# The last expert's rows joined to the final norm in PSUM, and the slots of extra rows made one step earlier

## The chip, the cores and the metric

One core of a Trainium2 chip runs one program. The metric is the device time of an execution in microseconds (us), shown as the median of three runs. All times below are of the kernel before, unless the text says otherwise.

## The reference

An encoder block on 1024 tokens of width 1024: time mixing and attention, then a top-4-of-32 expert layer, and a layer norm after each. Only its last part matters here:

```python
ffn = _moe(h, router_w, router_b, exp_w1, exp_b1, exp_w2, exp_b2)
h = _layer_norm(DEEPNORM_ALPHA * h + ffn, ln2_w, ln2_b)
# for each expert e and the rows xb that chose it:
hid = xb @ w1[e] + b1[e]                       # 1024 -> 2048
act = x_glu * sigmoid(1.702 * x_glu) * (x_lin + 1)   # both halves clamped
out = (act @ w2[e] + b2[e]) * gate             # 1024 -> 1024, summed over the experts of a token
```

## The kernel before, in words

**The expert stage** (`experts`) takes some 1,520 us of the program. The 32 experts are ranked by how many rows they got, and stand in a fixed order of places, `SEQ` (L42). The 18 fullest (ranks below `NH`) have room for 160 rows, 128 and 32 extra ones; the other 14 have room for 128. A place with room for extra rows is called an x place here, and the others plain. `SEQ` mixes both; with x for an x place and a dot for a plain one it reads `x.x.x.xx.x.x.x.xx.x.x.xx.x.x.xx.`. Rows beyond an expert's room go to a loop at the end (`For_i`, L1383) over blocks of left-over rows; its count comes from a register.

The stage runs in 32 windows. **Window r** is `up` of place r (8 blocks of weights, each with 12 products of 128x512 into the PSUM tile `h`) and then `down` of place r-1 (4 blocks, each with 12 products into `o`). Weights arrive as fp32 in a ring of six 1 MB buffers `raw`, and ACT and DVE split each block into a high part `wh` (a cast, L1177) and a low part `wl` (a subtraction, L1180). Extra rows have fp32 products of their own into `ex`: after every second block, eight of them at a time (L1198, L1253).

The small work is hung on 12 steps of a window, in a table `jobs` that is written by hand: step s comes after up block s (0 to 7) or after down block s-8 (8 to 11). An engine does its part in the order in which the steps are called. What matters here:

- Steps 8 and 9: the two halves of the activation of place r (`gm`, `lm` on DVE, `sm` on ACT), L1215 to L1219.
- Step 8 (`SLP` = -4), after the first half: `slots` for place r+2. PE makes the table of row numbers with one-hot products into a PSUM tile of tag `tr`; DVE copies it out as `sv` (and `st`, the extra rows' part) and works out the indices of the gather that POOL issues.
- Step 10 (`SLP + SLE` with `SLE` = 2), if place r+2 is an x place: `extra` (L1023). PE turns `st` with one product, `slots<-ident,st` (L1026), again into a `tr` tile, and DVE copies it out as a second `sv` (L1004).
- Step 11 and steps 1 and 2 of the next window (`TP`): the activation is transposed by PE into `tr` tiles (L1145, L1240), which ACT casts (`ah`) and DVE subtracts from (`al`, L1148).

There is one buffer of tag `tr`, so each of its users on PE waits until the one before has been copied out.

**The end of the stage.** `down` scales the rows by their gate (ACT, L1271) and POOL adds them to `ya_d` in DRAM with an indirect DMA (L1272; the extra rows L1281). These additions wait for one another. After window 31 comes `down` of the last place, alone, and then the loop over left-over blocks, at whose head all engines meet after every DMA has landed.

**The final norm** (`final_norm`) reads `ya_d` in eight tiles `fy` of 128x1024 and `ln2`'s weight and bias. DVE takes the statistics (L1444, L1446), subtracts the mean and multiplies by the weight (L1448), and works out the reciprocal root with a chain of small operations for two tiles at a time (L288 to L302). For five tiles ACT multiplies by the root (L1434) and POOL adds the bias (L1435); for the tiles in `FV` DVE does both (L1432).

Of the kernel before, what the change touches and what calls it, by code (L numbers as in the profile page):

```python
# [18 lines left out]
P = 128  # L19
# [19 lines left out]
CAP = P + CX  # L39
NH = 18  # L40

SEQ = (0, *sorted(range(1, NE - 1), key=lambda r: (r + 0.5) / NH if r < NH else (r - NH + 0.5) / (NE - NH)), NE - 1)  # L42

FIRST = 10
XP = (4, 5, 7)
TP = (11, 13, 14)
SLP = -4
SLE = 2
S1 = 1
MP = 6  # L50
DP = 8
# [1 line left out]
EH = 3  # L53

XB = 2
FG = (0, 2, 4, 6, 8)
FV = (4, 6, 7)
HB = 2
SB = 3
PB = 2  # L60
# [11 lines left out]
def hybrid_kernel(ctx: ExitStack, tc: tile.TileContext, A, out):  # L72
# [204 lines left out]
    ps3_.__exit__(None, None, None)  # L277
    p3_.__exit__(None, None, None)
    experts(tc, A, dict(locals()))
    final_norm(tc, A, dict(locals()))  # L280


def rsqrt_steps(nc, pool, v, n, scale, eps, name="rq", out=None):
# [830 lines left out]
def experts(tc, A, L):  # L1114
# [3 lines left out]
    with ExitStack() as cx:  # L1118
        wr = L["wr"]
        ep = cx.enter_context(tc.tile_pool(name="ep", bufs=1, reuse_waits="tile"))  # L1120
        wp = cx.enter_context(tc.tile_pool(name="wp", bufs=1, side="right", reuse_waits="tile"))
        pq = cx.enter_context(tc.tile_pool(name="pq", bufs=1, space=PS, reuse_waits="tile"))
        bh, ioc, select, pr = (L[k] for k in ("bh", "ioc", "select", "pr"))
        o = ep.tile([P, D], FT, name="o")
        ox = ep.tile([CX, 2, 512], FT, name="ox")
        def record(e, xtra):
            n = CAP if xtra else P
            pv = ep.tile([P, NT, 8], BF, name="pv", bufs=2)
            sp.dma_start(pv, L["val_d"][bass.ds(e, 1)].rearrange("e p t c -> p (e t) c"))
            return pv, n  # L1130

        def mark(pv, n, pos):
            oh = ep.tile([P, NT, CAP], BF, name="oh")[:, :, :n]
# [29 lines left out]

        stream, raws, highs, ready = [], L["raws"], L["highs"], []

        def weights(j, ahead):

            while len(raws) < min(j + RB, len(stream)):
                raw = wr.tile([P, 2 * FF], FT, name="raw", bufs=RB)
# [12 lines left out]
            return ready[j]  # L1182

        def up(j0, sel, xh, xl, xt, step=lambda s: None):
            ps = pq.tile([P, 4, 512], FT, name="h")
            px = pq.tile([P, 512], FT, name="ex") if xt is not None else None
            cols = [slice(512 * c, 512 * c + 512) for c in range(4)]
            for c, m in enumerate(cols):
                pe.matmul(ps[:, c], sel, bh[:, m], start=True, stop=False)

            def extra(k, raw):
                if px is None:
                    return
                if k == 0:
                    for c, m in enumerate(cols):
                        pe.matmul(px[32 * c:32 * c + 32], sel[:, 0:CX], bh[:, m], start=True, stop=False)
                for c, m in enumerate(cols):
                    pe.matmul(px[32 * c:32 * c + 32], xt[:, k], raw[:, m], start=False, stop=(k == KD - 1))  # L1198

            late = []  # L1200
            for k in range(KD):
                raw, h, l = weights(j0 + k, AH[xt is not None])
# [41 lines left out]
        def down(j0, ah, al, ax, gate, idx, step=lambda s: None):  # L1244
# [9 lines left out]

            late = []
            for b in range(4):
                raw, h, l = weights(j0 + b, AH[ax is not None])
                for kk in range(2):
                    k = 2 * b + kk
                    for x, w, z in ((ah, h, False), (ah, l, False), (al, h, k == KD - 1)):  # L1260
# [6 lines left out]
                        extra(*x)  # L1267
                    late.clear()
                step(KD + b)
            o = ep.tile([P, D], FT, name="o")  # L1270
            ac.activation(o, po.rearrange("p c n -> p (c n)"), AF.Copy, scale=gate[:, 0:1])  # L1271
            gp.indirect_dma_start(out=ya_d, out_offset=bass.IndirectOffsetOnAxis(ap=idx[:, 0:1], axis=0), in_=o, in_offset=None, compute_op=OP.add)  # L1272
            if px is None:
                return
# [31 lines left out]
        def begin2(r):  # L1306
            pv, n = info[r]
            info[r] = (pv, mark(pv, n, pv[:, :, 6:7]), n, select(L["pick"][:, SEQ[r]:SEQ[r] + 1]))

        def begin3(r, xs=None):  # L1310
            pv, oh, n, sel = info[r]
# [7 lines left out]
        def plan(r, where, f):  # L1319
            jobs.setdefault(12 * r + where, []).append(f)  # L1320
# [13 lines left out]
        with tc.manual_schedule():  # L1334
# [48 lines left out]
        with tc.For_i(0, n, 1) as i:  # L1383
            ei = ep.tile([1, 1], I32, name="ei")
            sp.dma_start(ei, L["tabi_d"][bass.ds(i, 1), :])
            row = L["tab_d"][bass.ds(i, 1), :]
# [14 lines left out]
            raws.clear()  # L1401
            highs.clear()
            ready.clear()
            parts, turns, a = act(*up(0, select(pick), *x))
            run_all(parts + turns)
            down(KD, *a, gate, idx)


def final_norm(tc, A, L):
    nc = tc.nc  # L1410
    ve, ac, gp, sp = nc.vector, nc.scalar, nc.gpsimd, nc.sync
    ya_d, bcast, out = L["ya_d"], L["bcast"], L["out"]
    with tc.tile_pool(name="fn", bufs=1, reuse_waits="tile") as fp:
        ys = [fp.tile([P, D], FT, name=f"fy{t}") for t in range(NT)]
        w = fp.tile([P, D], FT, name="l2w")
        b = fp.tile([P, D], FT, name="l2b")
        for t in range(NT):
            sp.dma_start(ys[t], ya_d[t * P:(t + 1) * P, :])  # L1418
            if t == 0:
                sp.dma_start(w, bcast(A["ln2_w"], D))  # L1420
            elif t == 4:
                sp.dma_start(b, bcast(A["ln2_b"], D))
        mv = fp.tile([P, NT, 2], FT, name="fmv")
        st = fp.tile([P, NT, 2, 6], FT, name="fst")
        def chain(g0, g1):
            return rsqrt_steps(nc, fp, mv[:, g0:g1, 1], g1 - g0, 1.0, LN_EPS, name=f"f{g0}")

        def last(g0, g1, r):
            for t in range(g0, g1):
                rt = r[:, t - g0:t - g0 + 1]  # L1430
                if t in FV:
                    ve.scalar_tensor_tensor(ys[t], ys[t], rt, b, op0=OP.mult, op1=OP.add)  # L1432
                else:
                    ac.activation(ys[t], ys[t], AF.Copy, scale=rt)  # L1434
                    gp.tensor_tensor(ys[t], ys[t], b, op=OP.add)  # L1435
                sp.dma_start(out[t * P:(t + 1) * P, :], ys[t])

        with tc.manual_schedule():
            run = None
            for g0, g1 in zip(FG, FG[1:]):  # L1440
                for t in range(g0, g1):
                    for i in range(4):
                        if i < 2:
                            ve.bn_stats(st[:, t, i], ys[t][:, 512 * i:512 * i + 512])  # L1444
                        elif i == 2:
                            ve.bn_aggr(mv[:, t], st[:, t])  # L1446
                        else:
                            ve.scalar_tensor_tensor(ys[t], ys[t], mv[:, t, 0:1], w, op0=OP.subtract, op1=OP.mult)  # L1448
                        if run is not None and next(run[0], run) is run:
                            last(*run[1:])  # L1450
                            run = None
                if run is not None:
                    for _ in run[0]:
                        pass
                    last(*run[1:])
                c = chain(g0, g1)
                run = (c, g0, g1, next(c))
            for _ in run[0]:
                pass
            last(*run[1:])  # L1460


def L_lor(lor, which):
# [55 lines left out]
```

## Time and profile before

| | us |
|---|---|
| median of 3 runs (2611.49 to 2621.80) | 2618.14 |
| the profiled execution | 2618.31 |
| its span | 2616.6 |
| PE busy | 2376.1 (91%) |
| DVE busy | 1940.6 (74%) |
| ACT busy | 1319.8 (50%) |
| POOL busy | 415.6 (16%) |
| mean granted TensorE clock | 0.961 of full speed |

The rows further down are of that profiled execution. In a view of time a row is: start, duration, engine, line of the kernel, operation, out<-in, sizes, count; a bracket at its end tells how long the engine had been idle and which instruction ended that. PE is the matmul engine and PEld its weight load; SPq is a DMA that SyncE's queue issues. In a view by stretches PEclk is the granted clock: 1.00 is 2.4 GHz and 0.50 is 1.2 GHz.

### The profile page before, as it was taken

The numbers are of one execution on the slowest core, as the hardware profiler recorded it, in microseconds if no ns is written. First come the engines' busy times: TensorE is split into PE (matmuls) and PEld (weight loads), VectorE is DVE, ScalarE is ACT, GpSimd is POOL, SyncE is SP. The second block draws the span as 40 slices with busy tenths as digits, with TensorE's granted clock in tenths as the row PEclk, the third lists the DMA queues.
The fourth block names the chain that finished last, engine by engine and source line by source line (L and its number), as shares of the span: only waits on it lengthen the run. The fifth ranks groups of instructions, "written<-read, shape, count | busy, mean of one in ns | idle before, by whom it ended". The sixth has DMA issues, their size and how long they took to land. (4 is left out here: it accounts for less than half of the span.)

```text
span 2616.6 us, 37332 instructions
## 1 busy us (share of the span) xinstructions
PE 2376.1 (91%) x14029; PEld 1793.9 (69%) x14029; DVE 1940.6 (74%) x2901; ACT 1319.8 (50%) x1606; POOL 415.6 (16%) x370
## 2 busy tenths in 40 slices
PE   5999998998989996899999999999999999999991
PEld 5778998977766664656666666666666666666660
DVE  8367344377886687778788887887878888788786
ACT  3354332354344333546556566565655656556561
POOL 4300211122131011011111011110211102102002
PEclk9999999999999996999999999999999999999995
DMA  6323864217537325677877779777897778977774
GB/s 225 130 81 143 278 204 71 93 51 255 172 125 268 111 86 180 259 261 277 323 286 286 298 272 339 283 258 294 305 337 273 272 284 310 330 277 266 287 276 155
DMA packets 184649, 607.14 MB, mean 232 GB/s; under 512 B 69961, under 2 KB 95689, under 8 KB 130834
## 3 DMA queue, kind: packets, MB, share of 16 engines
q1 hardware_dynamic: 155874, 525.24, 54.3%
q0 software_dynamic: 17600, 65.55, 9.0%
q10 hardware_dynamic: 10992, 13.93, 1.7%
q8 instruction: 112, 1.84, 0.3%
q14 instruction: 71, 0.58, 0.1%
HBM read 518.64 MB, written 86.02 MB: 231 GB/s over the span
## 5 line engine op out<-in xcount | busy, mean ns | idle before, releaser
L1180 DVE TENSOR_TENSOR wl<-raw,wh 128x2048 fp32r<-128x2048 f32 x384 | 876.1, 2289 | 223.3 <-ACT wh L1177 222.7
L1177 ACT CAST wh<-raw 128x2048 fp32r<-128x2048 f32 x381 | 720.9, 1905 | 127.5 <-DMA raw<-w 78.6
L1205 PE MATMUL h<-wh,xh 128*128 128x512 f32 x1024 | 307.5, 423 | 1.0 <-ACT wh L1177 1.0
L1205 PE MATMUL h<-wl,xh 128*128 128x512 f32 x1024 | 285.5, 401 | 1.1 <-DVE wl L1180 1.1
L1205 PE MATMUL h<-wh,xl 128*128 128x512 f32 x1024 | 281.1, 396 | 0.0
L1205 PEld LDWEIGHTS h<-wl,xh 128*128 128x128 f32 x1024 | 196.5, 192 | 49.3 <-DVE wl L1180 1.6
L1205 PEld LDWEIGHTS h<-wh,xh 128*128 128x128 f32 x1024 | 189.2, 195 | 56.0 <-issue 12.3
L1205 PEld LDWEIGHTS h<-wh,xl 128*128 128x128 f32 x1024 | 193.6, 189 | 47.1
L1009 POOL DMA_INDIRECT xg<-h_d,idx x32 | 70.4, 2202 | 955.9 <-PE ex L1253 307.6
L153 PE MATMUL mm<-whi,hT_lo 128*128 128x256 f32 x640 | 186.6, 293 | 10.4 <-DVE hT_lo L182 5.4
L151 PE MATMUL mm<-whi,hT_hi 128*128 128x256 f32 x640 | 186.9, 293 | 5.3 <-ACT sq L487 3.6
L152 PE MATMUL mm<-wlo,hT_hi 128*128 128x256 f32 x640 | 185.6, 291 | 0.0
L1263 PE MATMUL o<-wh,ah 128*128 128x512 f32 x512 | 170.9, 415 | 0.0
L1263 PE MATMUL o<-wl,ah 128*128 128x512 f32 x512 | 161.4, 396 | 0.0
L1263 PE MATMUL o<-wh,al 128*128 128x512 f32 x512 | 161.3, 396 | 0.0
L1216 ACT ACTIVATE sm<-gm 128x512 f32<-128x512 f32 x64 | 40.4, 632 | 199.8 <-DVE gm L1215 199.8
L1198 PE MATMUL ex<-raw,xt 128*32 128x512 f32 x1152 | 139.7, 603 | 0.0
L153 PEld LDWEIGHTS mm<-whi,hT_lo 128*128 128x128 f32 x640 | 126.2, 197 | 12.3 <-DVE hT_lo L182 6.6
L151 PEld LDWEIGHTS mm<-whi,hT_hi 128*128 128x128 f32 x640 | 126.5, 198 | 8.6 <-ACT sq L487 4.0
L152 PEld LDWEIGHTS mm<-wlo,hT_hi 128*128 128x128 f32 x640 | 126.3, 197 | 0.0
L1263 PEld LDWEIGHTS o<-wh,ah 128*128 128x128 f32 x512 | 89.1, 188 | 42.4 <-issue 25.1
L1263 PEld LDWEIGHTS o<-wh,al 128*128 128x128 f32 x512 | 96.4, 188 | 23.3
(421 smaller groups left out, 4154.3 us busy)
## 6 DMA issues: line engine op xcount, KB each, us to landing
raw<-w SPq DMA_DIRECT2D x384, 1024.0 KB, 7.0
pks<-pk_d SPq DMA_DIRECT2D x16, 1152.0 KB, 6.0
pk_d<-pk POOLq DMA_DIRECT2D x16, 896.0 KB, 5.4
h_d<-h SPq DMA_DIRECT2D x17, 512.0 KB, 2.6
raw<-w_fx ACTq DMA_DIRECT2D x8, 1024.0 KB, 5.4
fx_d<-fraw POOLq DMA_DIRECT2D x64, 128.0 KB, 2.8
qkvo<-fx_d SPq DMA_DIRECT2D x32, 256.0 KB, 6.1
x<-x SPq DMA_DIRECT2D x8, 512.0 KB, 3.8
```

The source lines that it names most:

```text
L151: pe.matmul(ps, hi[:, k, n], whi[:, k], start=(k == 0), stop=False)
L152: pe.matmul(ps, hi[:, k, n], wlo[:, k], start=False, stop=False)
L153: pe.matmul(ps, lo[:, k, n], whi[:, k], start=False, stop=(k == KD - 1))
L1009: gp.indirect_dma_start(out=x, out_offset=None, in_=h1_d, in_offset=bass.IndirectOffsetOnAxis(ap=idx[0:m, i:i + 1], axis=0))
L1177: ac.copy(highs[i], raw)
L1180: ve.tensor_tensor(l, raw, f32(h), op=OP.subtract)
L1198: pe.matmul(px[32 * c:32 * c + 32], xt[:, k], raw[:, m], start=False, stop=(k == KD - 1))
L1205: pe.matmul(ps[:, c], x[:, k], w[:, m], start=False, stop=z)
L1216: ac.activation(sg, g, AF.Sigmoid, scale=SWI)
L1263: pe.matmul(po[:, c], x[:, k], w[:, m], start=(k == 0 and x is ah and w is h), stop=z)
```

## The change

1. **`extra` moves from step 10 to step 9** (`SLE` = 1), and stands in front of what step 9 already held, the second half of the activation.
2. **The order of places**: the plain place of rank 30 moves to place 30, right before the last, which is plain too, and the others are mixed again. In the same signs the order is now `x.x.xx.x.xx.x.xx.x.xx.x.xx.x.x..`.
3. **The last place's rows are not added to `ya_d`.** They stay in SBUF (`kept[:, S:]`). PE turns the place's one-hot table `oh` (8 products with a bf16 unit matrix `idb`, copied out by ACT into `oht`), in front of the last `down`. The final norm then makes each tile in PSUM: two fp32 products of `ident` with the tile of `ya_d`, and two of `oht` with the kept rows, 128x512 each.
4. **The reads of `ya_d` move** in front of the last `down`, into four of the six `raw` buffers (`sums`, four DMAs of 1 MB), with the weight and the bias of the norm before them. They must follow the additions of place 30. The loop over left-over blocks is then in front of the norm; inside it, each turn reads the sums again.
5. **The norm itself**: DVE reads the tile from PSUM in three places (statistics twice, subtraction); the chain works in a PSUM tile `ch`, takes three, three and two tiles (`FG`), and has the factor -1/8192 moved into the weight (ACT, once). DVE finishes tiles 6 and 7 (`FV`) with the bias from PSUM, and ACT and POOL the other six.

```diff
-SEQ = (0, *sorted(range(1, NE - 1), key=lambda r: (r + 0.5) / NH if r < NH else (r - NH + 0.5) / (NE - NH)), NE - 1)
+SEQ = (0, *sorted(range(1, NE - 2), key=lambda r: (r + 0.5) / NH if r < NH else (r - NH + 0.5) / (NE - 2 - NH)), NE - 2, NE - 1)
-SLE = 2
+SLE = 1
-FG = (0, 2, 4, 6, 8)
-FV = (4, 6, 7)
+FG = (0, 3, 6, 8)
+FV = (6, 7)
...
                     if SEQ[r] < NH:
-                        plan(r - 1, (S1 if r == 1 else SLP) + SLE, extra)
+                        jobs.setdefault(12 * (r - 1) + (S1 if r == 1 else SLP) + SLE, []).insert(0, extra)
...
-            down(at["d", NE - 1], *prev)
+            ring = lambda: wr.tile([P, 2 * FF], FT, name="raw", bufs=RB)
+            kept = ring()
+            oht = kept[:, :S].rearrange("p (t q) -> p t q", t=NT)
+            for g in range(2):
+                ps = pq.tile([P, 4, P], FT, name="tr")
+                for j in range(4):
+                    pe.matmul(ps[:, j], last_oh[0][:, 4 * g + j], idb, start=True, stop=True)
+                ac.copy(oht[:, 4 * g:4 * g + 4], ps)
+            wb = ring().rearrange("p (i d) -> p i d", i=2)
+            for i, nm in enumerate(("ln2_w", "ln2_b")):
+                sp.dma_start(wb[:, i], L["bcast"](A[nm], D))
+            ys = [ring().rearrange("p (t d) -> p t d", t=2) for _ in range(NT // 2)]
...
+            sums()
+            down(at["d", NE - 1], *prev, o=kept[:, S:])
...
+    ac.activation(w, w, AF.Copy, scale=-1.0 / 8192.0)
+    def bring(t):
+        y = pt.tile([P, 2, 512], FT, name="y", bufs=3)
+        for c in range(2):
+            q = slice(512 * c, 512 * c + 512)
+            pe.matmul(y[:, c], ident, ys[t][:, q], start=True, stop=False)
+        for c in range(2):
+            q = slice(512 * c, 512 * c + 512)
+            pe.matmul(y[:, c], oht[:, t], o[:, q], start=False, stop=True)
+        return y
...
+    for g0, g1 in zip(FG, FG[1:]):
+        for t in range(g0, g1):
+            y = bring(t)
+            for c in range(2):
+                ve.bn_stats(st[:, t, c], y[:, c])
+                advance()
+            ve.bn_aggr(mv[:, t], st[:, t])
+            advance()
+            ve.scalar_tensor_tensor(ys[t], y.rearrange("p c n -> p (c n)"), mv[:, t, 0:1], w, op0=OP.subtract, op1=OP.mult)
+            advance()
+        advance(True)
+        run = (chain(g0, g1), g0, g1)
+        next(run[0])
```

`advance` does one small operation of the earlier group's chain, and calls `finish` (scale, bias, DMA out) when the chain has ended.

What the table does to the order is seen best on DVE, in `down` of a window whose place r+2 is an x place (L1215 to L1219 are one half of the activation, `wl` the low part of the next weights). Before:

```order
L1219 TENSOR_TENSOR lm<-lm,sm 128x512 [waits DVE_49,Activation_49]
L1029 COPY st<-slots 6x128 [waits PE_49]
L1004 COPY sv<-slots 128x6
...
L1180 TENSOR_TENSOR wl<-raw,wh 128x2048 [waits DMAHW7_49,Activation_49]
L1215 TENSOR_SCALAR gm<-h 128x512
L1217 TENSOR_SCALAR lm<-h 128x512
L1218 SCALAR_TENSOR_TENSOR lm<-lm,gm 128x512 [waits DVE_49]
L1219 TENSOR_TENSOR lm<-lm,sm 128x512 [waits DVE_49,Activation_49]
L1180 TENSOR_TENSOR wl<-raw,wh 128x2048 [waits DMAHW0_49,Activation_49]
L1004 COPY sv<-slots 128x6 [waits PE_49]
```

Now (L1028 is `st`, L1003 `sv`, L1187 `wl`, L1222 to L1226 the activation):

```order
L1226 TENSOR_TENSOR lm<-lm,sm 128x512 [waits DVE_49,Activation_49]
L1028 COPY st<-slots 6x128 [waits PE_49]
L1003 COPY sv<-slots 128x6
...
L1187 TENSOR_TENSOR wl<-raw,wh 128x2048 [waits DMAHW4_49,Activation_49]
L1003 COPY sv<-slots 128x6 [waits DVE_49,PE_49]
...
L1222 TENSOR_SCALAR gm<-h 128x512
L1224 TENSOR_SCALAR lm<-h 128x512
L1225 SCALAR_TENSOR_TENSOR lm<-lm,gm 128x512 [waits DVE_49]
L1226 TENSOR_TENSOR lm<-lm,sm 128x512 [waits DVE_49,Activation_49]
L1187 TENSOR_TENSOR wl<-raw,wh 128x2048 [waits DMAHW5_49,Activation_49]
```

The second `sv` has moved in front of the second half of the activation and of one `wl`.

On PE the product that waits for `st` and the transposes that need its `tr` tile stand in the same `down`; each block of weights is six pairs of products. Before, the three blocks ahead of it:

```order
L1263 MATMUL o<-wh,al 128x512 x2
L1263 MATMUL o<-wh,ah 128x512 x2
L1263 MATMUL o<-wl,ah 128x512 x2
L1263 MATMUL o<-wh,al 128x512 x2
L1026 MATMUL slots<-ident,st 128x6 [waits DVE_49,PE_49]
L1263 MATMUL o<-wh,ah 128x512 [waits Activation_49]
...
L1263 MATMUL o<-wh,al 128x512 x2
L1145 MATMUL tr<-ident,lm 128x128 [waits DVE_49]
```

Now, two blocks ahead of it and two behind:

```order
L1270 MATMUL o<-wh,al 128x512 x2
L1025 MATMUL slots<-ident,st 128x6 [waits DVE_49,PE_49]
L1270 MATMUL o<-wh,ah 128x512 [waits Activation_49]
...
L1270 MATMUL o<-wh,ah 128x512 [waits Activation_49]
...
L1270 MATMUL o<-wh,al 128x512 x2
L1149 MATMUL tr<-ident,lm 128x128 [waits DVE_49]
```

The product stands one block earlier on PE, and the transposes have one block more between it and them.

At the end of the stage, PE's rows between the last transposes of the activation and the last `down` are new:

```order
L1149 MATMUL tr<-ident,lm 128x128 [waits DVE_49]
L1149 MATMUL tr<-ident,lm 128x128 x3
L1399 LDWEIGHTS oh
L1399 MATMUL tr<-idb,oh 128x128 [waits DVE_49]
...
L1399 MATMUL tr<-idb,oh 128x128 [waits Activation_49]
...
L1270 MATMUL o<-wh,ah 128x512 x2
```

Each group of four waits until the `tr` tile before it has been copied out, by DVE and then by ACT.

## Rows read from the trace of the kernel before

**Rows 1.** The waits of PE: engine, line <- releaser: total us, times, longest.

```profile
PE tr L1145 <- DVE sv L1004: 45.5, 13, 4.8
...
PE tr L1240 <- DVE al L1148: 6.4, 4, 1.7
```

**Rows 2.** PE in time, the `down` of window 13 and the next `up`.

```profile
1504.27 0.63 PE L1263 MATMUL o<-wh,ah 128*128 128x512 f32 x2
...
1515.04 1.11 PE L1145 MATMUL tr<-ident,lm 128*128 128x128 f32 x4 [4.50 <-DVE sv L1004]
...
1524.93 0.60 PE L1145 MATMUL tr<-ident,lm 128*128 128x128 f32 x4
```

**Rows 3.** DVE in time, the same stretch.

```profile
1506.61 0.14 DVE L1004 COPY sv<-slots 128x6 f32<-128x6 f32 x1
...
1514.83 0.15 DVE L1004 COPY sv<-slots 128x6 f32<-128x6 f32 x1
```

**Rows 4.** All engines in time, window 5 (place 5 plain, 4 x).

```profile
1315.21 1.92 PE L1253 MATMUL ex<-raw,ax 128*32 128x512 f32 x16
...
1316.18 0.14 DVE L1004 COPY sv<-slots 128x6 f32<-128x6 f32 x1
```

**Rows 5.** PE in time, windows 7 (places 7 and 6 both x) and 8.

```profile
1421.29 0.66 PE L1145 MATMUL tr<-ident,lm 128*128 128x128 f32 x4 [0.61 <-DVE sv L1004]
...
1428.26 0.60 PE L1145 MATMUL tr<-ident,lm 128*128 128x128 f32 x4
...
1433.23 0.44 PE L1240 MATMUL tr<-ident,lx 128*128 128x128 f32 x2 [1.57 <-DVE al L1148]
```

**Rows 6.** Stretches from a wait's end on: us, PE busy, PEclk, DMA share, GB/s.

```profile
1186.50:1193.50 7.00, 7.00 (x26) 0.76 0.88 305
1515.00:1522.00 7.00, 6.96 (x20) 0.55 0.91 312
...
1433.20:1440.20 7.00, 6.97 (x33) 1.00 1.03 399
...
2545.60:2552.60 7.00, 6.95 (x26) 0.77 0.50 77
```

**Rows 7.** All engines in time, from window 31's end to the end.

```profile
2545.65 1.11 PE L1145 MATMUL tr<-ident,lm 128*128 128x128 f32 x4 [2.22 <-DVE al L1148]
...
2548.08 0.69 DVE L1148 TENSOR_TENSOR al<-tr,ah 128x512 fp32r<-128x512 f32 x1
...
2558.29 0.63 PE L1263 MATMUL o<-wh,al 128*128 128x512 f32 x2
2558.96 1.11 ACT L1271 ACTIVATE o<-o,gate 128x1024 f32<-128x1024 f32 x1 [9.16 <-PE o L1263]
...
2567.36 0.35 SPq L1418 DMA_DIRECT2D fy<-ya_d  x1
...
2570.99 1.29 DVE L1444 BATCH_NORM_STATS2 fst<-fy 128x6 f32<-128x512 f32 x2 [18.86 <-DMA fy<-ya_d]
...
2610.40 2.48 DVE L1432 SCALAR_TENSOR_TENSOR fy<-fy,f_r,l2b 128x1024 f32<-128x1024 f32 x2
```

**Rows 8.** POOL and DVE in time, the norm.

```profile
2595.50 4.63 POOL L1435 TENSOR_TENSOR fy<-fy,l2b 128x1024 f32<-128x1024 f32 x2 [5.92 <-ACT fy L1434]
...
...
2597.78 3.44 DVE L1448 SCALAR_TENSOR_TENSOR fy<-fy,fmv,l2w 128x1024 f32<-128x1024 f32 x1
...
2602.84 1.28 DVE L1448 SCALAR_TENSOR_TENSOR fy<-fy,fmv,l2w 128x1024 f32<-128x1024 f32 x1
```

**Rows 9.** PE in time, two fp32 products of 128x512 (L444, four records) behind another.

```profile
157.49 0.39 PE L146 MATMUL mm<-hT_hi,wlo 128*128 128x512 f32 x1
157.72 1.88 PE L444 MATMUL qk<-kn,bdones 128*128 128x512 f32 x4
```

**Rows 10.** POOL and DVE in time, an earlier stage: an addition beside one with a PSUM input.

```profile
929.96 2.36 POOL L328 TENSOR_TENSOR h<-h,p3lb 128x1024 f32<-128x1024 f32 x1 [21.12 <-DVE h L327]
...
930.25 0.67 DVE L908 TENSOR_TENSOR u<-u,mm 128x512 f32<-128x512 f32 x1
```

More of the change, by code (lines that the diff above doesn't have):

```diff
@@ L279, in hybrid_kernel @@
     experts(tc, A, dict(locals()))
-    final_norm(tc, A, dict(locals()))
 def rsqrt_steps(nc, pool, v, n, scale, eps, name="rq", out=None):
@@ L1121, in experts @@
         wp = cx.enter_context(tc.tile_pool(name="wp", bufs=1, side="right", reuse_waits="tile"))
-        pq = cx.enter_context(tc.tile_pool(name="pq", bufs=1, space=PS, reuse_waits="tile"))
+        pq_ = tc.tile_pool(name="pq", bufs=1, space=PS, reuse_waits="tile")
+        pq = pq_.__enter__()
+        idb = ep.tile([P, P], BF, name="idb")
+        ve.tensor_copy(idb, ident)
         bh, ioc, select, pr = (L[k] for k in ("bh", "ioc", "select", "pr"))
@@ L1130, in record @@
             return pv, n
+        last_oh = []
         def mark(pv, n, pos):
@@ L1164, in experts @@
         stream, raws, highs, ready = [], L["raws"], L["highs"], []
+        src = ["raw", RB, RB]
         def weights(j, ahead):
-            while len(raws) < min(j + RB, len(stream)):
-                raw = wr.tile([P, 2 * FF], FT, name="raw", bufs=RB)
+            while len(raws) < min(j + src[1], len(stream)):
+                raw = wr.tile([P, 2 * FF], FT, name="raw", tag=src[0], bufs=src[2])
                 sp.dma_start(raw, stream[len(raws)]())
@@ L1201, in up @@
             for k in range(KD):
-                raw, h, l = weights(j0 + k, AH[xt is not None])
+                raw, h, l = weights(j0 + k, AH[xt is not None] if src[0] == "raw" else 0)
                 for x, w, z in ((xh, h, False), (xh, l, False), (xl, h, k == KD - 1)):
@@ L1242, in act, with down @@
             return [extra, lambda: half(0), lambda: half(1)], turns + [piece], (ah, al, ax)
-        def down(j0, ah, al, ax, gate, idx, step=lambda s: None):
+        def down(j0, ah, al, ax, gate, idx, step=lambda s: None, o=None):
             po = pq.tile([P, 2, 512], FT, name="o")
@@ L1256, in down @@
             for b in range(4):
-                raw, h, l = weights(j0 + b, AH[ax is not None])
+                raw, h, l = weights(j0 + b, AH[ax is not None] if src[0] == "raw" else 0)
                 for kk in range(2):
@@ L1269, in down @@
                 step(KD + b)
-            o = ep.tile([P, D], FT, name="o")
+            keep = o is not None
+            if not keep:
+                o = ep.tile([P, D], FT, name="o")
             ac.activation(o, po.rearrange("p c n -> p (c n)"), AF.Copy, scale=gate[:, 0:1])
+            if keep:
+                return
             gp.indirect_dma_start(out=ya_d, out_offset=bass.IndirectOffsetOnAxis(ap=idx[:, 0:1], axis=0), in_=o, in_offset=None, compute_op=OP.add)
@@ L1308, in begin2 @@
             info[r] = (pv, mark(pv, n, pv[:, :, 6:7]), n, select(L["pick"][:, SEQ[r]:SEQ[r] + 1]))
+            if r == NE - 1:
+                last_oh.append(info[r][1])
         def begin3(r, xs=None):
@@ L1378, in experts, with sums @@
                 step(NE, s)
-            down(at["d", NE - 1], *prev)
+            ring = lambda: wr.tile([P, 2 * FF], FT, name="raw", bufs=RB)
[10 more added lines that the diff above has]
+            ys = [ring().rearrange("p (t d) -> p t d", t=2) for _ in range(NT // 2)]
+            def sums():
+                for g, y in enumerate(ys):
+                    sp.dma_start(y, ya_d[2 * g * P:2 * (g + 1) * P, :].rearrange("(t p) d -> p t d", p=P))
+            sums()
+            down(at["d", NE - 1], *prev, o=kept[:, S:])
+            pq_.__exit__(None, None, None)
         n = nc.values_load(L["tot"][0:1, 0:1], min_val=0, max_val=NE)
         with tc.For_i(0, n, 1) as i:
+            pq_ = tc.tile_pool(name="pq2", bufs=1, space=PS, reuse_waits="tile")
+            pq = pq_.__enter__()
             ei = ep.tile([1, 1], I32, name="ei")
@@ L1403, in experts @@
             ready.clear()
+            src[:] = "wh", 2, WB
             parts, turns, a = act(*up(0, select(pick), *x))
@@ L1406, in experts @@
             down(KD, *a, gate, idx)
-def final_norm(tc, A, L):
-    nc = tc.nc
[L1411 to L1460, printed above, removed]
@@ new lines, in experts, with final_norm, chain, finish @@
+            sums()
+            pq_.__exit__(None, None, None)
+        with tc.manual_schedule(), tc.tile_pool(name="pt", bufs=1, space=PS, reuse_waits="tile") as pt:
+            final_norm(tc, A, L, ep, pt, wb, [y[:, t] for y in ys for t in range(2)], oht, kept[:, S:])
+def final_norm(tc, A, L, ep, pt, wb, ys, oht, o):
+    nc = tc.nc
+    ve, ac, pe, gp, sp = nc.vector, nc.scalar, nc.tensor, nc.gpsimd, nc.sync
+    out, ident = L["out"], L["ident"]
+    w, b = wb[:, 0], wb[:, 1]
+    ac.activation(w, w, AF.Copy, scale=-1.0 / 8192.0)
+    mv = ep.tile([P, NT, 2], FT, name="fmv")
+    st = ep.tile([P, NT, 2, 6], FT, name="fst")
+    rr = ep.tile([P, NT], FT, name="frr")
+    def bring(t):
[7 more added lines that the diff above has]
+        return y
+    def chain(g0, g1):
+        n = g1 - g0
+        tl = pt.tile([P, 2, 8], FT, name="ch")
+        a, t = (tl[:, i, 0:n] for i in range(2))
+        r = rr[:, g0:g1]
+        ve.tensor_scalar(a, mv[:, g0:g1, 1], LN_EPS, None, op0=OP.add)
+        yield
+        ve.tensor_scalar(r.bitcast(I32), a.bitcast(I32), -0.5, 1597463007.0, op0=OP.mult, op1=OP.add)
+        yield
+        for c in (3.0, 12.0, 768.0):
+            ve.tensor_tensor(t, a, r, op=OP.mult)
+            yield
+            ve.tensor_tensor(t, t, r, op=OP.mult)
+            yield
+            ve.scalar_tensor_tensor(r, t, c, r, op0=OP.subtract, op1=OP.mult)
+            yield
+    def finish(g0, g1):
+        for t in range(g0, g1):
+            rt = rr[:, t:t + 1]
+            if t in FV:
+                ve.scalar_tensor_tensor(ys[t], ys[t], rt, bp[0].rearrange("p c n -> p (c n)"), op0=OP.mult, op1=OP.add)
+            else:
+                ac.activation(ys[t], ys[t], AF.Copy, scale=rt)
+                gp.tensor_tensor(ys[t], ys[t], b, op=OP.add)
+            sp.dma_start(out[t * P:(t + 1) * P, :], ys[t])
+    run, bp = None, []
+    def advance(to_end=False):
+        nonlocal run
+        while run is not None:
+            if next(run[0], run) is run:
+                finish(*run[1:])
+                run = None
+            if not to_end:
+                return
+    for g0, g1 in zip(FG, FG[1:]):
+        for t in range(g0, g1):
+            y = bring(t)
[9 more added lines that the diff above has]
+        next(run[0])
+    bp.append(pt.tile([P, 2, 512], FT, name="y", bufs=3))
+    for c in range(2):
+        pe.matmul(bp[0][:, c], L["ons"][0:1], wb[0:1, 1, 512 * c:512 * c + 512], start=True, stop=True)
+    advance(True)
```

## The prediction

> **What bounds the kernel now.** I read the page first: PE is busy for 91% of the span, so the time is PE's products plus PE's waits, and behind the last product comes a tail without PE. The waits of PE, grouped by releaser, say which waits are worth anything: the largest of the whole program is that of the transposes `tr<-ident,lm` for DVE's `sv`, 45.5 us in 13 waits [rows 1]. The reader should then see one such wait in time. In window 13 PE ends its last `down` block, sits 4.5 us and starts the transposes at 1515.04, when the second `sv` has been copied at 1514.83 [rows 2, 3]. They share one `tr` buffer, and two `wl` and half an activation stand ahead of that copy on DVE. Nine of the 13 waits are of this kind: x places with a plain one before them and an x place two further on. Three last 0.6 us, in windows whose place and the one before are both x [rows 5], where the extra rows' products give DVE time; one, in window 0, lasts 2.7. The stretches behind the waits show a second price: over the 7 us from a 4.5 us wait on, the granted clock is 0.55 (six of the nine are near this) or 0.76 (the other three), and 1.00 from a wait of 1.57 on [rows 6]. Time behind the end of a wait is lost as well, then. At the end, 57.7 us lie between the last product at 2558.9 [rows 7] and the span's end at 2616.6.
>
> The profiled execution (2618.31) is practically the median (2618.14), so the sum stands against both.
>
> **Term 1, the wait for `sv`: -27.** `slots<-ident,st` now stands one block earlier, after the second block of `down`. PE reaches that place at 1504.27 in window 13 [rows 2], but the first `sv`, which frees `tr`, ends only at 1506.75 [rows 3]. So a wait of 2.5, with the release 2.6 us, appears there. The new order has six windows of this kind (x place, plain before, x two further on). Where the place before is x, PE first has extra products until 1317.13, and `sv` is copied at 1316.3 [rows 4]: no wait, if the window's own place is plain. Where both are x (five windows), I take the 0.6 of the old wait [rows 5]; its bounds are 0 and 2.6. The wait of window 0 goes, as its `extra` also moves ahead of the work it stood behind. The second `sv` now waits for no `wl` that PE's transposes could feel: it has 5 us less in front of it. 6 x 2.6 + 5 x 0.6 = 18.6 against 45.5: **-26.9**.
>
> **Term 2, the extra rows' transposes, late next: +6.** `tr<-ident,lx` waits for DVE's `al`: 6.4 us in four waits [rows 1], 1.57 each behind a pair of x places [rows 5]. The new order has five such pairs. In the six windows of term 1 PE comes earlier than before, and a wait of between 0 and 1.57 is new; I take 0.8. 5 x 1.57 + 6 x 0.8 - 6.4 = **+6.3**; the lower bound is no growth, 0.
>
> **Term 3, the clock: -12.** From the first transposes to the second PE takes 9.89 us behind a 4.5 us wait [rows 2] and 6.97 undisturbed [rows 5]: 2.9 lost. Where the stretch shows 0.76, a quarter of 7 us is lost: 1.7. Six and three of them make 22.5 us, which go with the long waits. The question is what a wait of 2.6 does. A wait of 1.57 leaves the clock at 1.00; the nearest one, 2.22 before the last transposes [rows 7], is followed by 0.77 [rows 6], the low level of 1.2 GHz for some 3 us. So I let each of the six waits cost 1.7: 10.2 instead of 22.5, **-12.3**. Bounds: no fall at all (10.2 less), or 2.9 each (7.2 more).
>
> **Term 4, the seam before the last `down`: +7.** Place 30 is now plain. Its two groups of extra products, 2 x 1.92 us [rows 4], are made in another window, but the second transposes at 2545.65 waited for DVE, not for PE [rows 7], and stay where they are: +3.8, at least 0 if DVE follows PE. Behind them comes new work. The one `tr` buffer is free when DVE's `al` ends at 2548.77 [rows 7]; then four products, ACT's copy and four more. With 0.4 us for each four (a little less than the 0.6 of four fp32 transposes [rows 2]) and 0.8 for the copy with its waits, the last `down` starts at 2550.4 instead of 2546.8, where the transposes end: +3.6. Together **+7.4**.
>
> **Term 5, behind the last product: -11.** Before, 57.7 us. After: ACT scales the rows, 1.1 [rows 7]; the engines meet, 1.0 (before, scale, addition, landing and meeting took 8.4 from the last product to the first read [rows 7], so it is at most 7.3). The reads of 4 MB are behind nothing but place 30's addition: in the times before, PE's work ahead of the second transposes ends by 2543.4, plus 1.1 and 7.3 they start by 2551.8, and at 399 GB/s [rows 6] they have landed by 2562.3, while the last `down` now ends at 2562.5. They are hidden, with nothing to spare. PE has idled some 2 us by then, so I add one fall of the clock, 1.7. Then eight tiles of four fp32 products: two such products took 1.88 with the pipeline's tail, and single ones that follow each other 0.23 apart last 0.39 [rows 9], so the tail is 0.16 and one product costs 0.86 (at most 0.94). 32 x 0.86 = 27.5. DVE needs about 3.1 per tile (statistics 1.3, their sum 0.2, subtraction 1.3, four small ones), less than PE's 3.45, and hides. After PE, DVE has the last tile, 2.8, and the rest of the second group's chain, 0.6; then ACT 1.1, POOL three additions of 2.32 [rows 8], 7.0, and the last transfer 3.7 (from DVE's end at 2612.88 to the span's [rows 7]). The two tiles that DVE finishes are done before POOL's. 1.1 + 1.0 + 1.7 + 27.5 + 2.8 + 0.6 + 1.1 + 7.0 + 3.7 = 46.5: **-11.2**.
>
> This takes for granted that POOL no longer holds DVE up. Before, beside POOL's additions, the subtraction took 3.44 instead of 1.28 [rows 8]. An addition of DVE with one input in PSUM took 0.67 for half the elements under a POOL addition [rows 10], so it was not held up, and every large operation of the new norm has one input in PSUM. The Trainium skill ("GPSIMD Engine Reference", section 8, "Key points") says that POOL shares its SBUF interfaces with VectorE and that the two get into each other's way when VectorE reads two SBUF inputs or uses a two-port mode; by that rule nothing waits here, and the trace agrees. Were the rule wider than that, four operations of DVE would wait 2.2 us each (an estimate), and the sum would be 8.6 us worse.
>
> **Sum:** -26.9 + 6.3 - 12.3 + 7.4 - 11.2 = -36.7, from 2618.3: **2582**. Alone, its bounds are 2560 (no fall in terms 3 and 5, no growth in term 2, 3.8 less in term 4) and 2609 (2.9 for each fall, products of 0.94, a meeting of 7.3, 2.6 in the five windows of term 1); few of these come together.
>
> **Rivals.**
> (a) *The norm's products at the low clock.* The engines meet first, PE's product of each tile may pause for a free buffer, and if the clock stays at 1.2 GHz through the norm, 32 products cost 27.5 more, less the 1.7 already counted: 2608. For it: 0.50 to 0.77 after pauses [rows 6]. Against: PE has no pause between tiles as long as DVE is faster. The Trainium skill ("TensorE: Matmul & The Clock Gate", "What's actually happening") says that the throttled clock is the default state and activity releases it; by that the norm's own activity releases it, which is against this rival.
> (b) *The wait moves whole.* If DVE is as late at the new place as at the old, six waits of 4.5 with falls of 2.9 stand there: 6 x (1.9 + 1.2) = 18.6 more, 2601. For it: the first `sv` is behind half an activation that needs ACT. Against: 1506.61 [rows 3].
> (c) *The step's move does nothing.* If the transposes wait as long as before, because DVE's second `sv` stays late, terms 1 to 3 are nothing: 2618.3 + 7.4 - 11.2 = 2615. Against: the order on DVE, where the copy now stands ahead of the second half and a `wl`.
> (d) *Slower: many short waits each drop the clock.* The new order has fewer long waits but more short ones: 16 of about 0.6 to 1.6 us besides the six. At 2.9 for each, 16 x 2.9 + 7.2 = 53.6 more: 2636. It decides for slower once about all of them fall. Against: 1.00 behind the wait of 1.57 [rows 5, 6].
>
> **How the numbers follow.** My forecast has 0.72, (b) 0.10, (a) 0.08, (c) 0.06, (d) 0.04. The predicted time is the forecast's 2582. The range, 2558 to 2608, takes in the forecast's own bounds, (b) and (a); outside are (c), (d) and what the bounds miss. No change within 0.5% means 2605 to 2631, about what a measurement of this kernel can tell. Nearly all of the forecast and most of (b) lie below: faster 0.80; (c), most of (a) and a forecast gone wrong in two terms: same 0.16; (d): slower 0.04.
>
> **What would show it.** Right: among PE's waits, `tr` for `sv` is gone and `slots<-ident,st` for `sv` has six of about 2.6; PEclk behind each is near 0.76; the reads of `ya_d` are issued before the last `down` ends; the norm's products come 0.86 apart, DVE's subtraction stays at 1.28 beside POOL, and POOL's additions end last. Wrong: waits of 4 us and more at the new place, DVE's copies waiting for PE, PEclk of 0.50 through the norm, a first norm product much more than 3 us behind the last `down`, or a subtraction of 3.4 us.

## The result, and the profile after

The changed kernel takes 2585.86 us (median; 2580.36 to 2586.71) against 2619.97 of the kernel before on the same chip; the ratio is 0.9862, 95% interval 0.9844 to 0.9880. That is faster by 1.4%, and 4 us above the 2582 that was predicted, inside the range of 2558 to 2608. The profiled execution has a span of 2584.9 us, 31.7 less than before, and a mean granted clock of 0.967 instead of 0.961.

PE's waits after the change (engine, line <- releaser: total us, times, longest). They answer to [rows 1]:

```profile
PE slots L1025 <- DVE sv L1003: 24.7, 12, 6.1
...
PE tr L1247 <- DVE al L1152: 11.0, 7, 1.8
...
PE tr L1149 <- DVE al L1152: 6.6, 2, 6.3
...
PE tr L1149 <- DVE sv L1003: 0.3, 1, 0.3
```

The largest wait of before, 45.5 us of the transposes for `sv`, is gone but for 0.3. The product `slots<-ident,st` now waits for it: 24.7 us in 12 waits. One of them, 6.05 in window 0, stood there before too; the other eleven sum to 18.6, six of about 2.5 (one of these is 3.2) and five of 0.6.

Two of the six in time (PE; the transposes of the same `down` behind each), and the stretches from three of the waits' ends on, with two of the norm below them (us, PE busy, PEclk, DMA share, GB/s). They answer to [rows 2, 6]:

```profile
1410.92 0.35 PE L1025 MATMUL slots<-ident,st 6*128 6x6 f32 x2 [2.46 <-DVE sv L1003]
...
1416.90 0.60 PE L1149 MATMUL tr<-ident,lm 128*128 128x128 f32 x4
...
1641.38 0.35 PE L1025 MATMUL slots<-ident,st 6*128 6x6 f32 x2 [2.46 <-DVE sv L1003]
...
1648.92 0.60 PE L1149 MATMUL tr<-ident,lm 128*128 128x128 f32 x4
```

```profile
1179.50:1186.50 7.00, 7.00 (x24) 0.76 0.97 377
1410.90:1417.90 7.00, 6.98 (x33) 1.00 0.95 364
1641.40:1648.40 7.00, 7.00 (x24) 0.76 0.94 363
2535.80:2542.80 7.00, 6.99 (x13) 0.76 0.01 2
2542.80:2564.00 21.20, 21.20 (x51) 1.00 0.00 1
```

These transposes wait for nothing now. The same 2.46 us cost more at one place than at the other: the work from the wait's end to the transposes takes 7.54 us behind the wait that ends at 1641.38, and only 5.98 behind the one at 1410.92. The difference of 1.56 goes with a granted clock of 0.76 and of 1.00. Five of the six waits are followed by the longer time.

The end of the program, all engines in time; it answers to [rows 7, 8]:

```profile
2515.80 1.11 PE L1149 MATMUL tr<-ident,lm 128*128 128x128 f32 x4 [6.27 <-DVE al L1152]
...
2518.32 0.59 PE L1399 MATMUL tr<-idb,oh 128*128 128x128 bf16 x4 [1.40 <-DVE al L1152]
...
2519.58 0.58 PE L1399 MATMUL tr<-idb,oh 128*128 128x128 bf16 x4 [0.67 <-ACT raw L1400]
...
2519.92 1.20 PE L1270 MATMUL o<-wh,ah 128*128 128x512 f32 x2
...
2521.33 3.96 SPq L1408 DMA_DIRECT2D raw<-ya_d  x4
...
2531.86 0.63 PE L1270 MATMUL o<-wh,al 128*128 128x512 f32 x2
...
2535.82 3.59 PE L1464 MATMUL y<-raw,ident 128*128 128x512 f32 x4 [3.32 <-SPq L1415]
...
2541.05 1.88 PE L1464 MATMUL y<-raw,ident 128*128 128x512 f32 x4
...
2561.17 6.96 POOL L1495 TENSOR_TENSOR raw<-raw 128x1024 f32<-128x1024 f32 x3 [44.59 <-ACT raw L1494]
...
2563.49 1.28 DVE L1517 SCALAR_TENSOR_TENSOR raw<-y,fmv,raw 128x1024 f32<-128x1024 f32 x1
...
2568.78 3.23 ACT L1494 ACTIVATE raw<-raw,frr 128x1024 f32<-128x1024 f32 x3 [5.62 <-DVE frr L1485]
2570.01 6.96 POOL L1495 TENSOR_TENSOR raw<-raw 128x1024 f32<-128x1024 f32 x3 [1.88 <-ACT raw L1494]
```

From the last product of `down`, which ends at 2532.49, to the end of the span are 52.4 us, where 57.7 stood. POOL's last addition ends at 2576.97, 8 us ahead of the end. The prediction had 3.7 there. Two views show what the 8 us are: the last transfers out that SyncE's queue issues, and the instructions that end the program, by queue (least, median and longest duration in ns, first and last start):

```profile
2574.70 3.94 SPq L1496 DMA_DIRECT2D out<-raw  x4
```

```profile
L1580 POOLq DRAIN  x3: 46/109/12038, 2572.1 to 2584.7; - x3
L1580 SPq DRAIN  x3: 7/7/13, 2582.5 to 2584.3; - x3
```

POOL's queue drains for 12.0 us, from 2572.1 to 2584.1: it is done 7.1 us after POOL's last addition. SyncE's queue sends the tiles in their order, so three of the last four are issued behind that addition, from 2577.00 on; it has waited for all and drains at 2582.5, 1.6 us ahead of POOL's queue. The end follows 0.8 us behind the later of the two.

### The profile page after: what moved, and what is told of

It reads as the page before. It is cut to its first block, busy times and chain, and to the rows that moved or that the text cites. A ratio compares the mean times of both kernels' runs of the same rounds, so it can differ in the third digit from the quotient of the medians.

```text
span 2584.9 us, 37479 instructions
## 1 busy us (share of the span) xinstructions
PE 2401.8 (93%) x14105; PEld 1809.5 (70%) x14105; DVE 1928.6 (75%) x2886; ACT 1322.4 (51%) x1610; POOL 397.7 (15%) x370
## 5 line engine op out<-in xcount | busy, mean ns | idle before, releaser
L1187 DVE TENSOR_TENSOR wl<-raw,wh 128x2048 fp32r<-128x2048 f32 x384 | 873.8, 2289 | 195.8 <-ACT wh L1184 194.8
L1212 PE MATMUL h<-wh,xh 128*128 128x512 f32 x1024 | 299.4, 414 | 1.7 <-ACT wh L1184 1.7
L1212 PEld LDWEIGHTS h<-wh,xh 128*128 128x128 f32 x1024 | 184.0, 190 | 53.7 <-ACT wh L1184 9.6
L153 PEld LDWEIGHTS mm<-whi,hT_lo 128*128 128x128 f32 x640 | 126.6, 198 | 11.2 <-DVE hT_lo L182 5.8
L1270 PEld LDWEIGHTS o<-wh,ah 128*128 128x128 f32 x512 | 92.1, 193 | 34.9 <-issue 15.1
```

Source lines behind the costliest of these rows:

```text
L153: pe.matmul(ps, lo[:, k, n], whi[:, k], start=False, stop=(k == KD - 1))
L1270: pe.matmul(po[:, c], x[:, k], w[:, m], start=(k == 0 and x is ah and w is h), stop=z)
```

## The experiments

My theory was that the stage carries the gain, through shorter waits and the clock behind them, and that the new end of the program gives almost nothing. The rivals: the order of places carries it, or the new end does. Each ratio below is to the kernel before.

**The step alone.** The kernel before with

```diff
-SLE = 2
+SLE = 1
...
-                        plan(r - 1, (S1 if r == 1 else SLP) + SLE, extra)
+                        jobs.setdefault(12 * (r - 1) + (S1 if r == 1 else SLP) + SLE, []).insert(0, extra)
```

> The kernel before with the step of `extra` alone (SLE 1, in front of the second half of the activation); order of places and end of the program as before. My theory, that the gain of the stage is the shorter wait and the clock behind it: nine waits of about 2.5 us at the new place and none of 4.5 at the transposes, three of 0.6, the wait of 2.7 in window 0 gone: 21 us less; granted clock 0.76 over 7 us behind most of the nine, which costs 9 x 5/6 x 1.7 = 13 instead of 22.5: 10 less; together about 30 us less than the kernel before. Rival, that the order of places carries the gain and the step only moves the wait: within 8 us of the kernel before.

Measured: 2590.23 us, ratio 0.9885 (0.9860 to 0.9909), 30 us less. Its waits, in the line numbers of the kernel before:

```profile
PE slots L1026 <- DVE sv L1004: 30.4, 13, 6.0
...
PE tr L1240 <- DVE al L1148: 8.4, 6, 2.0
```

Without window 0's 6.0 that is 24.4 instead of 45.5: the 21 us of the theory. Seven of its nine waits of 2.5 are followed by the longer time, 1.5 each.

**The order alone.** The kernel before with the new `SEQ`.

> The kernel before with the new order of places alone. My theory: six waits of 4.5 us instead of nine and five of 0.6 instead of three, 12.5 less; the clock behind them 6 x 2.5 instead of 22.5, 7.5 less; transposes of extra rows 3 more; 3.8 more in front of the last down, where place 30 is plain; together about 13 us less than the kernel before. Rival, that the order carries the gain: 25 to 30 us less.

Measured: 2610.99 us, ratio 0.9968 (0.9954 to 0.9983), 8 us less, under the theory's 13 and far from the rival's 25 to 30.

```profile
PE tr L1145 <- DVE sv L1004: 32.8, 12, 4.5
...
PE tr L1240 <- DVE al L1148: 9.5, 6, 1.6
...
PE tr L1145 <- DVE al L1148: 6.6, 2, 6.3
```

The waits are as expected, 12.7 less for `sv` and 3.1 more for `al`; the 6.3 is the seam in front of the last `down`, 2.2 before. In the two traces the missing 4 us lie ahead of the first window, where the programs are alike: the first transposes of `lm` come at 1086.2 here and at 1082.6 before. Over the eleven traces they come between 1080.6 and 1087.2, so a few us between two single traces can be of that part.

**Both, with the old end.**

> Both, and the end of the program as before: the change without its part on the last expert's rows and the norm. From the trace of the changed kernel the stage up to the last transposes is 30 us shorter than before, the last down starts 3.4 us later behind them than before, and what follows its last product takes 52.5 instead of 57.7 us. So my theory gives about 30 us less than the kernel before here, and only some 2 us more than that for the whole change. Rival, that the new end of the program carries a good part: 10 to 20 us less than before, and a clearly faster changed kernel.

Measured: 2587.42 us, ratio 0.9878 (0.9851 to 0.9906), 32 us less. The whole change has 0.9862, inside that interval. So the order adds little to the step (3 us between the medians), and rows joined in PSUM, reads moved forward and the new norm add little to both: between the two traces 1.6 us.

**What sets the end.** The changed kernel with four tiles finished by DVE; the bias is put into PSUM in front of the second group's end.

```diff
-FV = (6, 7)
+FV = (4, 5, 6, 7)
...
```

> The changed kernel with four tiles finished by DVE (4 to 7) instead of two, so that POOL has four additions instead of six. In the changed kernel POOL's last addition ends at 2576.97, POOL's drain at 2584.09, 7.1 us later, and the span at 2584.9; the last transfer out has landed by 2582.3. My theory, that the drain of POOL sets the end and follows its last addition by about 7 us: POOL ends 4.6 us earlier, DVE's last tile is ready at about 2576.0 and its transfer lands some 4 to 5 us later, so the end comes about 4 us earlier. Rival, that the transfers out set the end: 1.3 us or less, since SyncE's queue sends them in order of the tiles. All of it too small for the times, to be read in the profile from the last product on.

Measured: 2584.52 us, ratio 0.9866 (0.9840 to 0.9892), no difference in the times, as expected. In the trace (DVE and POOL in time, then the draining of the two queues):

```profile
2568.60 1.28 DVE L1517 SCALAR_TENSOR_TENSOR raw<-y,fmv,raw 128x1024 f32<-128x1024 f32 x1
...
2571.68 2.35 POOL L1495 TENSOR_TENSOR raw<-raw 128x1024 f32<-128x1024 f32 x1 [1.86 <-ACT raw L1494]
...
2575.05 2.47 DVE L1492 SCALAR_TENSOR_TENSOR raw<-raw,frr,y 128x1024 f32<-128x1024 f32 x2
```

```profile
L1581 POOLq DRAIN  x3: 46/109/9505, 2571.6 to 2582.7; - x3
L1581 SPq DRAIN  x3: 7/7/13, 2582.1 to 2582.4; - x3
```

POOL's last addition ends at 2574.03 and the drain at 2581.1, again 7.1 later. From the end of DVE's last subtraction (2569.88) to the span's end (2583.0) are 13.1 us; in the changed kernel 16.7 (2568.21 to 2584.9). 3.6 us less, where the theory had about 4. POOL's last addition and its drain both came 4.6 us earlier by the same measure, but SyncE's queue, which waits for the transfers out, drains only at 2582.1, 1.0 behind POOL's: so POOL's drain set the end of the changed kernel, and here the transfers set it. The norm's first product also came 2.1 us behind PE's last work here and not 3.3, and the clock stayed at 1.00 over its first 7 us.

**The wait that is left.** In the changed kernel DVE copies `st` and `sv` only behind half an activation. This kernel exchanges the two jobs of step 8.

```diff
-                for i in range(2):
-                    jobs.setdefault(12 * r + DP + i, []).insert(0, parts[i - 2])
+                plan(r, DP, parts[-2])
+                jobs.setdefault(12 * r + DP + 1, []).insert(0, parts[-1])
```

> The changed kernel with the two jobs of step 8 in the other order on DVE and PE: `slots` for place r+2 (the copies `st` and `sv`) in front of the first half of the activation. The product `slots<-ident,st` should then find its operand and the free `tr` buffer: in the changed kernel DVE starts the half at 1407.70 and `st` only at 1410.43, where PE arrived at 1408.46. My theory: the waits of 2.46 and 0.6 (18.6 us) go, and with them the falls of the clock behind five of them (1.6 each, 8 us); but PE then reaches the transposes of extra rows 4 us earlier in six windows and 0.6 earlier in five, and these wait for DVE's `al`, which comes no earlier: 2.5 to 2.8 in eleven windows instead of 1.8 in five, 20 us more, perhaps with falls of their own. Together 0 to 8 us less than the changed kernel. Rival, that the wait for `sv` is a cost by itself: 25 us less.

Measured: 2593.82 us, ratio 0.9888 (0.9863 to 0.9912): no gain, and 8 us more than the changed kernel by the medians, where the theory had 0 to 8 less. Its waits, and the stretches behind two of those for `al`:

```profile
PE tr L1247 <- DVE al L1152: 26.1, 12, 2.9
...
PE h L1196 <- DVE lm L1224: 7.2, 8, 1.1
...
PE slots L1025 <- DVE sv L1003: 3.3, 1, 3.3
```

```profile
1339.00:1346.00 7.00, 6.63 (x23) 0.76 1.01 417
...
1431.70:1438.70 7.00, 6.97 (x33) 1.00 1.03 358
```

The waits for `sv` are gone but for window 0's. 15.1 us of them stand at the transposes of extra rows now, and 7.2 (1.0 in the changed kernel) at the products that need `lm` read out, which the theory had not named. Two of the five waits of 2.9 have a lower clock behind them; the waits of 1.6 have none. From the first transposes of `lm` to the last window's the trace is 5.8 us longer than the changed kernel's: with the start of the next one, the six windows that lost the wait of 2.5 are together 2.1 us shorter, and the five with a pair of x places 7.4 longer, of which the two falls of the clock are some 2.8.

**The next job moved as well.** The same with the transposes of extra rows one block later, and four tiles by DVE.

```diff
-TP = (11, 13, 14)
+TP = (11, 13, 15)
...
```

> The same, with the transposes of extra rows one block later (step 3 of the next window instead of 2) and four tiles of the norm finished by DVE. My theory: PE has 3.3 us more ahead of these transposes, so the waits of 2.5 to 2.8 for `al` are gone too, and the gain of the stage comes through: 20 to 26 us less than the changed kernel for the stage and 3.6 for the end of POOL's drain. Rival, that DVE is late for the whole of the next window: the wait comes back at the transposes of `xg` or at the products for `wl`, and less than 10 us remain.

Measured: 2560.84 us, ratio 0.9759 (0.9729 to 0.9788): 25 us less than the changed kernel by the medians, inside the theory's 24 to 30.

```profile
PE tr L1149 <- DVE al L1152: 8.8, 8, 6.3
...
PE tr L1149 <- DVE xl L1152: 7.5, 6, 3.8
```

The wait for `al` at the extra rows is gone. At the transposes of `xg`, where the rival had it, come back five waits of 0.74, 3.7 in all.

**The later transposes alone.** The changed kernel with the new `TP` only.

> The changed kernel with the transposes of extra rows at step 3 of the next window instead of step 2, and nothing else. It tells whether slots_first_lx_late owed its 26 us to both moves together. My theory: the five waits of 1.8 and the one of 1.63 for `al` go (11 us), the six of 2.46 and the falls of the clock behind them stay: 6 to 11 us less than the changed kernel, so that some 12 us come only with both moves. Rival, that this step alone carries the gain: 20 us less.

Measured: 2579.41 us, ratio 0.9843 (0.9819 to 0.9867), 6 us less by the medians, as the theory has it. The sum of the two moves alone, +8 and -6, is far from the 25 less that they give together (of which 3.6 are the end's).

**The seam before the last `down`.** Two tries. One moves the block that makes `oht` in front of the last transposes, into the wait of 6.3 us, and to another PSUM bank (on top of `slots_first` and four tiles by DVE):

```diff
-                ps = pq.tile([P, 4, P], FT, name="tr")
+                ps = pq.tile([P, 4, P], FT, name="ex")
...
```

> The first of these with four tiles of the norm finished by DVE, and with the eight products of the last place's one-hot table moved into PE's wait of 6.3 us ahead of the last transposes, in the PSUM bank of the extra rows instead of `tr`. My theory: the last down starts 3.3 us earlier behind the last transposes (0.8 instead of 4.1), but the reads of ya_d still wait for place 30's addition, so PE waits up to 3 us longer for the meeting of the engines, and at most 1 us of it shows at the end. Rival, that the seam is on the path: the first product of the norm comes 3 us earlier.

Measured: 2592.67 us, ratio 0.9884 (0.9862 to 0.9906). PE in time, with the reads of `ya_d`, the seam and the norm's start:

```profile
2516.07 0.60 PE L1149 MATMUL tr<-ident,lm 128*128 128x128 f32 x4
2516.51 0.39 PE L1396 MATMUL ex<-idb,oh 128*128 128x128 bf16 x4
...
2521.95 0.59 PE L1396 MATMUL ex<-idb,oh 128*128 128x128 bf16 x4 [5.06 <-ACT raw L1397]
...
2529.87 2.10 SPq L1407 DMA_DIRECT2D raw<-ya_d  x4
...
2544.48 3.78 PE L1463 MATMUL y<-raw,ident 128*128 128x512 f32 x4 [7.09 <-SPq L1414]
```

The last `down` starts 3.1 us earlier behind the first transposes (8.0 us instead of 11.1 in `slots_first`), as the theory has it, and the wait for the meeting grows to 7.1: from the first transposes to the norm are 28.4 us, 27.5 in `slots_first`. Nothing of the seam shows at the end. The reads of `ya_d` are issued 13.8 us behind the first transposes, where it was 12.3, and the meeting waits for them.

The other try adds to `slots_first_lx_late` that the weights of the last `down` are split behind the rows of place 30 and the last activation (`hold` is set for the `down` of place 30 alone), and keeps the first try's move:

```diff
-                raw, h, l = weights(j0 + b, AH[ax is not None] if src[0] == "raw" else 0)
+                raw, h, l = weights(j0 + b, 0 if src[0] != "raw" else min(AH[ax is not None], 3 - b) if hold else AH[ax is not None])
...
```

> slots_first_lx_late with another seam in front of the last down: the one-hot products in the bank of the extra rows during PE's wait, and no weights of the last down split ahead during the down before it, so that on ACT and DVE the scaling of place 30's rows and the first `ah` and `al` stand in front of them. My theory: the second transposes come 4 to 5 us earlier (DVE's two `wl` no longer stand ahead of `al`), place 30's addition is issued 3 us earlier and so are the reads of ya_d; PE's last down starts earlier but runs at the pace of DVE's `wl` (four of 2.3 us); the norm's first product comes 3 to 4 us earlier counted from the first transposes of the last window (26.1 in slots_first_lx_late), and the time is some 3 us shorter. Rival, that the split of the last weights takes the place of the wait: the last down ends no earlier, and the norm starts within 1 us of before.

Measured: 2561.14 us, ratio 0.9773 (0.9752 to 0.9794), the same as without. PE in time, and two stretches:

```profile
2486.36 0.60 PE L1149 MATMUL tr<-ident,lm 128*128 128x128 f32 x4
...
2489.35 0.61 PE L1149 MATMUL tr<-ident,lm 128*128 128x128 f32 x4
...
2492.47 1.22 PE L1270 MATMUL o<-wh,ah 128*128 128x512 f32 x2 [2.52 <-ACT wh L1184]
...
2495.82 1.05 PE L1270 MATMUL o<-wh,al 128*128 128x512 f32 x2
```

```profile
2492.40:2501.00 8.60, 7.42 (x17) 0.51 0.77 242
2501.00:2508.00 7.00, 7.00 (x32) 1.00 0.93 349
```

The second transposes came 3.9 us earlier (3.0 instead of 6.9 behind the first), but the first 8.6 us of the last `down` ran at 0.51 of the clock: a row of two products lasts 1.05 us, where 0.63 stood [rows 7]. From the first transposes to the norm 1.8 us were left of it, where the theory had 3 to 4. Neither theory had the lower clock.

## Why the prediction was right

**Term 1** (-26.9): 18.6 instead of 45.5 us, -26.9; six waits of 2.5 (one 3.2) and five of 0.6. The step alone gave the 21 us that were expected of it, too. **Right**, and with it rivals (b) and (c) fall.

**Term 2** (+6.3): 11.0 against 6.4, +4.6. The five pairs of x places wait 1.8 each, and the last x place, in whose window no product waits for `st`, 1.6; in the six windows of term 1, where 0.8 was taken, five have nothing and one 0.4. The wait ahead of them and the lower clock behind it had already made PE late there: the one with 0.4 is the one whose clock did not fall. `slots_first` shows it from the other side: without these, 2.9 stand behind the pairs and 1.6 in the six windows.

**Term 3** (-12.3): the six waits cost five times 1.55, 7.8 us, where 10.2 were taken; the nine of before cost 20.9 (each window's time between its transposes against the 6.96 of an undisturbed one), where 22.5 were taken. That is -13.1. In five kernels with this wait 26 of 33 have the lower clock behind them. Nothing in these runs says which ones.

**Term 4** (+7.4, of which 3.8 and 3.6): the wait for `al` grew from 2.22 to 6.27, and from the second transposes to the last `down` are 4.12 us instead of 0.77: +4.05 and +3.35, +7.4.

**Term 5** (-11.2): 52.4 instead of 57.7, -5.3. This is the step that failed. The parts: scale and meeting 3.3 where 2.1 stood, since the reads were not hidden in this execution: the last was issued at 2524.9 and took 9.5 us, so it landed some 2 us behind PE's last product, and the norm's first product was released by SyncE's queue; 32 products with one fall of the clock 29.4, where 29.2 stood; DVE's last tile and chain 3.4, ACT 1.3, POOL 7.0, nearly as predicted. But "the last transfer 3.7" was taken from an end that DVE had set, with one tile left to send. With POOL last, the end came 8.0 behind its last addition, 4.3 more. Of these, 2.7 are the transfers: DVE's two tiles were done, but stood behind POOL's in the order of sending, so SyncE's queue was done 5.5 us behind POOL's addition, where it was 2.8 behind DVE's last operation before (its first DRAIN at 2615.7). The other 1.6 are POOL's drain, which was done later still. Before, it was done at 2615.6, level with the transfers:

```profile
L1515 POOLq DRAIN  x3: 46/109/9573, 2606.0 to 2616.3; - x3
L1515 SPq DRAIN  x3: 7/7/13, 2615.7 to 2616.0; - x3
```

`four_by_dve` shows both: fewer additions moved POOL's end and its drain by the same 4.6 us, and the program's end by 3.6, up to the end of the transfers.

That POOL no longer holds DVE up was right: the subtraction at 2563.49 takes 1.28 us beside POOL's additions, where 3.44 stood [rows 8]. The Trainium skill ("GPSIMD Engine Reference", section 8, "Key points") has POOL and VectorE contend when VectorE reads two SBUF inputs or uses a two-port mode; this operation reads one input from PSUM, and the trace agrees.

Rival (a) was not there: 0.76 over the norm's first 7 us and 1.00 from then on. The Trainium skill ("TensorE: Matmul & The Clock Gate", "What's actually happening") has the clock released by activity, and the rows agree. Rival (d) was not either: behind the waits of 1.6 to 1.8 for `al` the work up to the transposes of `xg` takes 5.85 to 5.88 us in all six cases of the changed kernel and all seven of `slots_first`, where 5.81 stand in such windows without a wait; one of the six in `step_and_order` took 7.42, and 7.41 stand behind one of 1.93 in `step_only`, so such a fall is possible there, but rare.

The measured sum is -26.9 + 4.6 - 13.1 + 7.4 - 5.3 = -33.3, the difference of the spans -31.7; part of what is left is that the first wait of the stage ends at 1081.38 instead of 1079.32, behind work that both kernels share. That the time came within 4 us of the forecast owes something to luck: term 5 was 5.9 short, and terms 2 and 3 came out 2.5 better than taken. The parts that cost the program code most, the join in PSUM and the norm, are worth 2 us net: 5.3 gained behind the last product, 3.35 given back in front of the last `down`; between the traces of `step_and_order` and of the whole change it is 1.6.

## What to carry to other kernels

A wait on the bounding engine is priced with the clock behind it: here 2.5 us of waiting cost 4 in most places, and a row of the granted clock behind each wait tells which. Removing a wait alone can give nothing, because the engine that was late is late again one job further on, as in `slots_first`; move the next job too, and measure both together. Whoever gives the last work of a program to POOL should add what its queue needs to drain (7.1 us here), and see which results are still to be sent behind it.

## What was not expected of the hardware

- POOL's drain at the program's end was done 7.1 us behind POOL's last addition in the changed kernel (2576.97 and 2584.1) and in `four_by_dve` (2574.03 and 2581.1). In the kernel before the 7.2 us from POOL's last addition (2608.38) to the end of its drain (2615.58) ran beside DVE's last tiles and their transfers, which were done 0.1 us later (2615.7).
- Equal waits are not equally priced: 2.46 us are followed over 7 us by a clock of 0.76 at 1641 and of 1.00 at 1411 of the same execution.
- A last `down` whose products had to wait twice for their weights, 2.5 and 1.1 us, behind a wait of 1.9 at the one-hot products, ran its first 8.6 us at 0.51 of the clock (`seam`), although PE was busy for 7.4 of them.
